# Gated DeltaNet mixer: triangular inverse without interleaving, convolutions in half-k passes, one 512-wide z weight, later correction chains; sliding-window mixer: v and the first q as one weight

## The chip, the cores and the metric

The kernel runs on one core of one Trainium2 chip. The metric is device time of one execution in microseconds (us). Engines are called as in the profile: PE multiplies matrices, DVE is the vector engine, ACT the scalar engine, POOL the GpSimd engine, SP issues the weight transfers. Each runs its instructions strictly in its own order, and semaphores tie the engines together.

## The reference

A trunk of two layers on 256 tokens of width 1024, each layer a half-weighted SwiGLU, a mixer, and another half-weighted SwiGLU. The mixer of layer 0 is a gated DeltaNet, that of layer 1 is sliding-window attention.

```python
def mixer_gated_deltanet(h, ...):
    proj = h @ w_in                       # q, k, v, z of 1024 columns each, b and a of 8
    qkv = silu(causal_depthwise_conv(qkv, w_conv))     # 4 taps along the tokens
    q = l2norm(q) * 128 ** -0.5 ; k = l2norm(k)        # 8 heads of 128
    beta = sigmoid(b) ; g = -exp(A_log) * softplus(a + dt_bias)
    o = gated_delta_rule_chunked(q, k, v, g, beta)
    return (rmsnorm(o, out_norm) * silu(z)) @ w_out

def gated_delta_rule_chunked(...):        # per chunk: decay = exp(g_i - g_j), i >= j
    L = where(strict, (kb @ k.T) * decay, 0)            # kb = k * beta
    u, w = solve_unit_lower(L, [v * beta, kb * exp(g)]) # the kernel builds the inverse
    v_new = u - w @ S ; o = q_dec @ S + ((q @ k.T) * decay) @ v_new
    S = S * g_last + k_dec.T @ v_new

def mixer_sliding_window_sinks(h, ...):   # 16 query heads of 64, 4 key/value heads
    proj = h @ w_in + b_in                # q 1024, k 256, v 256 columns
```

The kernel works with chunks of 128 tokens, so there are two (`t` is 0 or 1).

## The kernel before

**Weights.** Every weight is used in near fp32: SP loads a piece of 512 KB into `raw` (4 buffers), ACT casts it to `whi` (L310), and DVE subtracts, `wlo = raw - whi` (L312). For a few pieces POOL does that in four slices of 256 elements (L317); the argument `npool` says for how many of the two pieces of a 256-column weight. `whi` and `wlo` have 5 buffers each. A projection of 256 columns is two pieces: k (the contraction, in 8 blocks of 128) 0 to 3, and 4 to 7. Each block takes three matmuls: high by high, high by low, low by high (lines 363 to 365).

**PSUM.** `psA` has four banks and holds what is being accumulated by projections (`pcv` in the convolutions, `pz`, `acc`), `psB` four banks for the small products.

**Gated DeltaNet (`gdn`).** The order of the source is: z columns in chunks of 256 (`zproj`), the gates, then `conv` for k chunks 0 to 3, v chunks 0 to 3 and q chunks 0 to 3, where a chunk is 256 columns, two heads. A `conv` projects its two halves of 128 columns one after the other, each through all 8 blocks into a `pcv` bank. ACT copies the bank, scaled by the last tap, to `cv`; three *taps* on DVE (L928, on 255, 254 and 253 elements) read the bank and add to `cv`; ACT applies Silu. The bank is free after the third tap. Side work is written as generators and handed to a `Ticker`, which runs one step of it after each half of a `conv`.

The k chunks feed the *inverse*. `kpost` transposes k (`pkn`), sums its squares with four accumulating activations (`sumsq`, L721) and multiplies k by k (`pkk`) into `nf`. `blocks` cuts out the 32x32 diagonal blocks (`d`; ACT copies, POOL multiplications L768 and L770). `inverse` inverts 16x16 blocks on DVE, lines 780 to 818, all heads at once, and ends in `yx`. Two chains (`chain(0)` and `chain(1)`, four heads each) then go to 32, 64 and 128 rows by small matmuls (`pt`, `py`, `px`), each followed by a copy on ACT or DVE. The chains feed `u_of` and `state`. The tail takes four outputs `po` (chunk t, head group g) through `post` (square on ACT L1051, sum on DVE L1052, power on POOL L1055, scaling by four DVE instructions L1057 to `on`), `turn` (transpose `poT`, cast `oT`), and the output projection `acc`.

**Order.** A scheduler puts the written instructions of all engines in an order by its own estimates; `issue_after` and `keep_in_program_order` pin some of them.

**Sliding-window (`swa`).** v (`pv`) and q's first 256 columns (`pq`) are two weights of 256.

Of the kernel before, what the change touches and what calls it, by code (L numbers as in the profile page):

```python
# [15 lines left out]
P = 128  # L16
# [197 lines left out]
class Kern:  # L214
    def __init__(self, ctx, tc):
        self.tc = tc
        self.nc = tc.nc
        self.cp = ctx.enter_context(tc.tile_pool(name="const", bufs=1))
        self.wp = ctx.enter_context(tc.tile_pool(name="wts", bufs=5))
        self.bp = ctx.enter_context(tc.tile_pool(name="big", bufs=11))  # L220
        self.sp = ctx.enter_context(tc.tile_pool(name="small", bufs=2))
        self.pp = ctx.enter_context(
            tc.tile_pool(name="ps", bufs=4, space=bass.MemoryType.PSUM)
        )
        self.consts()
        self.hold = None
        self.early = None

# [59 lines left out]
    def split(self, src, hi, lo, shape, eng=None, cuts=1):  # L288
        nc = self.nc
        raw = self.wp.tile(shape, F32, tag="raw", name="raw", bufs=4)  # L290
        n = shape[1] // cuts
        parts = [slice(i * n, (i + 1) * n) for i in range(cuts)]
        if len(src.shape) == 4:
            for k in range(shape[1]):
                nc.sync.dma_start(out=raw[:, k].rearrange("p (g f) -> p g f", g=2), in_=src[:, k])
        else:
            nc.sync.dma_start(out=raw, in_=src)
        with ExitStack() as behind:
            if self.hold is not None:
                self.hold[0] -= 1  # L300
                if self.hold[0] < 0:
                    for ins in self.hold[2:]:
                        behind.enter_context(self.tc.issue_after(ins.ins))
                elif self.early is not None:
                    behind.enter_context(self.tc.issue_after(self.early.ins))
                self.hold[1] -= 1
                if not self.hold[1]:
                    self.hold = self.early = None
            for c in parts:
                nc.scalar.copy(hi[:, c], raw[:, c])  # L310
                if eng is None:
                    nc.vector.tensor_tensor(out=lo[:, c], in0=raw[:, c], in1=hi[:, c].bitcast(F32), op=ALU.subtract)  # L312
            if eng is not None:

                r, h, l = (a.rearrange("p a b -> p (a b)").rearrange("p (n f) -> p n f", f=256) for a in (raw, hi, lo))
                for i in range(4):
                    eng.tensor_tensor(out=l[:, i], in0=r[:, i], in1=h[:, i].bitcast(F32), op=ALU.subtract)  # L317
# [10 lines left out]
    def wcols(self, w, c0, npool=0):  # L328
        src = w[:, c0:c0 + 256].rearrange("(k p) f -> p k f", p=P)
        pieces = [self.wpiece(src[:, 4 * i:4 * i + 4, :], 4, 256,  # L330
                              eng=self.nc.gpsimd if i >= 2 - npool else None) for i in range(2)]
        return lambda k, cs: tuple(a[:, k % 4, cs] for a in pieces[k // 4])

    def wpairs(self, w, c0, between=None):
# [3 lines left out]
        for i in range(4):  # L338
# [4 lines left out]
            if between is not None and i == 1:  # L343
                between()
        return lambda k, cs: tuple(a[:, k % 2, cs] for a in pieces[k // 2])
# [34 lines left out]
    def proj_T(self, out, w, f, nrm):  # L380
        fs = slice(f * P, (f + 1) * P)
        for k in range(KT):
            wh, wl = w(k, fs)
            self.mm3(out, wh, wl, nrm.h.hi(k), nrm.h.lo(k), k == 0, k == KT - 1)
# [296 lines left out]
    def gdn(self, nrm, prep, w_in, w_out, after):  # L681
# [9 lines left out]
        tk = Ticker()  # L691
        Dt = self.big([P, NT, H, P], "Dt")
# [32 lines left out]
        def kpost(c):  # L725
# [3 lines left out]
            nc.scalar.copy(kd[:, hs, :], pv[:, 0])  # L729
            nc.scalar.copy(keg[:, hs, :], pv[:, 1])  # L730
            sumsq(pv, ssk, 2 * c)
            yield
            beta, eG, eS = res["beta"], res["eG"], res["eS"]
# [7 lines left out]
            a = ssk[:, :, hs]  # L741
            nc.vector.tensor_scalar_add(a, a, EPS)
            nc.vector.reciprocal(br[:, :, hs], a)
            nc.vector.tensor_mul(br[:, :, hs], br[:, :, hs], beta[:, :, hs])
            nc.vector.tensor_scalar_mul(nbr[:, :, hs], br[:, :, hs], -1.0)
            yield
            nc.gpsimd.tensor_tensor(out=kd[:, hs, :], in0=kd[:, hs, :], in1=bc(eS, 0, hs), op=ALU.mult)
            nc.gpsimd.tensor_tensor(out=keg[:, hs, :], in0=keg[:, hs, :], in1=bc(eG, 1, hs), op=ALU.mult)
# [7 lines left out]
        def blocks(g):  # L756
# [4 lines left out]
            us = slice(8 * g, 8 * g + 8)  # L761
            raw = self.y1([P, 8, 32], "d32")
# [6 lines left out]
            for j, m in enumerate(("tri16", "off16")):  # L769
                nc.gpsimd.tensor_tensor(out=d2[:, j, us, :], in0=raw,  # L770
                                        in1=M[m].unsqueeze(1).to_broadcast([P, 8, 32]), op=ALU.mult)
            nc.gpsimd.tensor_tensor(out=sv[:, :, gs], in0=ssk[:, :, gs],
                                    in1=self.phalf.rearrange("p (t h) -> p t h", t=NT), op=ALU.pow)

        def inverse():
# [21 lines left out]
            yield  # L797
# [13 lines left out]
            yield  # L811
# [6 lines left out]
            nc.vector.transpose(yx[:, 1].rearrange("p u c -> p (u c)"), yx[:, 0].rearrange("p u c -> p (u c)"))  # L818
            late["yx"] = yx
            tk.add(chain(0), chain(1))  # L820

        def chain(g):
# [6 lines left out]
            def blockwise(ps, lhsT, rhs):  # L829
                for i in range(8):  # L830
                    for b in range(4):
                        bs = slice(32 * b, 32 * b + 32)
                        nc.tensor.matmul(ps[bs, i * 32:i * 32 + 32], lhsT=lhsT[bs, i, :], rhs=rhs[bs, i, :],
                                         start=True, stop=True)
# [15 lines left out]
            for i in range(8):  # L850
                for b in (0, 2):
                    e, o = slice(32 * b, 32 * b + 32), slice(32 * b + 32, 32 * b + 64)
                    nc.tensor.matmul(pt[o, i * 32:i * 32 + 32], lhsT=nf[e, i, o], rhs=X[e, i, :], start=True, stop=True)
# [8 lines left out]
            for i in range(8):  # L862
                for b in (0, 2):
                    e, o = slice(32 * b, 32 * b + 32), slice(32 * b + 32, 32 * b + 64)
                    nc.tensor.matmul(py[e, i * 32:i * 32 + 32], lhsT=t32[o, i, :], rhs=Y[o, i, :], start=True, stop=True)
# [52 lines left out]
        def conv(col0, dst, npool, start):  # L918
            w = self.wcols(w_in, col0, npool)
            for f in range(2):  # L920
                ct = col0 // P + f
                ps = self.psA("pcv")
                self.proj_T(ps[:, :T], w, f, nrm)
                c = self.c1([P, T], "cv")
                nc.scalar.activation(c, ps[:, :T], AF.Copy, scale=wc[:, 3, ct:ct + 1])
# [5 lines left out]
                with self.tc.issue_after(res["exp"].ins):  # L931
                    nc.scalar.activation(dst(f), c, AF.Silu)
                tk.tick()
            tk.add(*start, first=True)

        def zproj(c, t, w):
            pz = self.psA("pz")
            self.proj_N(pz[:, :T], w, t, nrm)
            hs = slice(2 * c, 2 * c + 2)
            nc.scalar.copy(zs[:, t, hs, :], pz[:, :T].rearrange("p (h c) -> p h c", h=2))  # L940

        def zgate(t, hs, keep=lambda ins: ins):
            z = zs[:, t, hs]
            keep(nc.scalar.activation(z, z, AF.Silu))
            keep(nc.gpsimd.tensor_tensor(
                out=z, in0=z, in1=onb.unsqueeze(1).to_broadcast([P, hs.stop - hs.start, P]), op=ALU.mult))
# [7 lines left out]
        def then(*steps):  # L954
            for st in steps:
                r = st()
                if r is not None:
                    yield from r
                    yield

        w = [self.wcols(w_in, 3 * D + c * 256) for c in range(2)]
        zproj(0, 0, w[0])
        zproj(1, 0, w[1])
        tk.add(self.gdn_gates(nrm, wabh, wabl, expA, dtb, Dt, wq, res))
        tk.tick()
        for c in range(2):
            zproj(c, 1, w[c])
            tk.tick()
        zc = [2]

        def zmore(n):
            for c in range(zc[0], zc[0] + n):
                w = self.wcols(w_in, 3 * D + c * 256)
                for t in range(NT):
                    zproj(c, t, w)
                    tk.tick()
# [3 lines left out]
        for c in range(4):  # L980
# [5 lines left out]
            conv(D + c * 256, lambda f: kT[:, 2 * c + f, :], c // 2, [then(*steps)])  # L986
# [94 lines left out]
        for c in range(4):  # L1081
# [5 lines left out]
            if c == 2:  # L1087
                n = 2 * zc[0]
                w = self.wcols(w_in, 3 * D + 3 * 256)
                for t in range(NT):  # L1090
                    zproj(3, t, w)
                    zgate(t, slice(n, H))
                    tk.tick()
        tk.drain()
# [53 lines left out]
    def swa(self, nrm, prep, w_in, w_out, after):  # L1148
# [9 lines left out]
        wv = self.wcols(w_in, D + 256)  # L1158
        w0 = self.wcols(w_in, 0)
        for t in range(NT):  # L1160
            ts = slice(t * P, (t + 1) * P)
            ps = self.psA("pv")
            self.proj_N(ps[:, :T], wv, t, nrm)
            nc.vector.tensor_add(v[:, t, :], ps[:, :T], bv)
            ps = self.psA("pq")
            self.proj_N(ps[:, :T], w0, t, nrm)
            qn = self.c1([P, T], "qn")
            nc.scalar.copy(qn, ps[:, :T])
            pt = self.psB("pqt")
# [205 lines left out]
```

## Time and profile before

| | |
|---|---|
| three runs, us | 1018.77, 1019.48 (median), 1020.96 |
| the profiled execution's own time, us | 1017.73 |
| its span, first to last instruction, us | 1016.0 |
| mean granted TensorE clock | 0.996 |
| busy: PE, DVE, ACT, POOL | 98%, 63%, 54%, 24% |
| gated DeltaNet, first `pz` matmul to the first matmul of the next SwiGLU, us | 195.39 to 368.90 |

All times on the trace's clock are us from the span's start. In a timeline row the first number is the start, the second how long it took; matmuls overlap, so the distance between starts says how long PE was held. The square bracket tells how long the engine stood idle before and for whom. PEclk is the clock granted to PE as a share of full speed.

### The profile page before, as it was taken

The page shows a single profiled execution, that of the slowest core. Times are in us where ns is not written, and L with a number is a line of the kernel's source. Part 1 is how long each engine was busy: PE and PEld are TensorE (multiplying, and loading weights), DVE is VectorE, ACT ScalarE, POOL GpSimd, SP SyncE. Part 2 cuts the span into 40 slices and gives each one's busy share as a digit, 9 for nine tenths or more (in the row PEclk, how much of TensorE's full clock was granted, in tenths as well). Part 3 has the DMA queues.
Part 4 walks back from the last instruction along what each step waited for, and adds up shares of the span by engine and source line. Part 5 has one row for each costly group of instructions (what it writes and reads, how often), then busy time and mean ns, then how long its engine had stood idle before and what let it go on. Part 6 is the DMA issues. An engine that isn't in the chain of part 4 may idle for free.

```text
span 1016.0 us, 16483 instructions
## 1 busy us (share of the span) xinstructions
PE 998.0 (98%) x6195; PEld 870.7 (86%) x6195; DVE 643.7 (63%) x975; ACT 547.8 (54%) x979; POOL 242.1 (24%) x311
## 2 busy tenths in 40 slices
PE   8999999999989999999999999999999999999997
PEld 7888888899979888888888888888898678888886
DVE  5866654666895766666546666664578756666544
ACT  5756544457856445555434655553467545555442
POOL 0125510017952301323100123320021402222100
PEclk9999999999999999999999999999999999999999
DMA  7766666644452337666666666665563426666661
GB/s 246 235 188 191 200 197 182 205 129 148 133 175 65 105 104 208 195 188 197 191 199 190 186 187 186 192 207 189 185 209 104 152 91 212 190 189 187 203 188 43
DMA packets 135316, 177.05 MB, mean 174 GB/s; under 512 B 7250, under 2 KB 120260, under 8 KB 135236
## 3 DMA queue, kind: packets, MB, share of 16 engines
q1 hardware_dynamic: 132032, 171.46, 55.3%
q10 hardware_dynamic: 3204, 4.53, 1.4%
q8 instruction: 49, 0.80, 0.3%
q14 instruction: 31, 0.25, 0.1%
HBM read 174.92 MB, written 1.05 MB: 173 GB/s over the span
## 4 chain that ended last, share of the span: by engine, by line
PE 89%; DVE 4%; ACT 3%; issue 1%; DMA 1%; POOL 1%; SPq 1%; POOLq 0%; ACTq 0%
PE pg L370 14%; PE pu L370 14%; PE acc L365 9%; PE acc L363 9%; PE acc L364 9%; PE pu L371 7%; PE pg L371 7%; PE pgu L365 2%; PE pgu L364 2%; PE pgu L363 2%; DVE wlo L312 1%; DMA raw<-in_ffn_w_gu_dram 1%; PE pcv L363 1%; PE pcv L364 1%; PE pcv L365 1%
## 5 line engine op out<-in xcount | busy, mean ns | idle before, releaser
L312 DVE TENSOR_TENSOR wlo<-raw,whi 128x1024 fp32r<-128x1024 f32 (+1 forms) x304 | 374.9, 1236 | 198.0 <-ACT whi L310 196.8
L310 ACT CAST whi<-raw 128x1024 fp32r<-128x1024 f32 (+1 forms) x318 | 330.3, 1046 | 179.5 <-PE acc L365 83.2
L370 PE MATMUL pg<-hs,whi 128*128 128x512 f32 x624 | 218.7, 392 | 0.0
L370 PE MATMUL pu<-hs,whi 128*128 128x512 f32 x624 | 218.4, 392 | 0.0
L371 PE MATMUL pu<-hs,wlo 128*128 128x256 f32 x624 | 175.4, 281 | 0.0
L371 PE MATMUL pg<-hs,wlo 128*128 128x256 f32 x624 | 174.6, 281 | 0.0
L478 POOL TENSOR_TENSOR act<-act,gate 128x256 f32<-128x256 f32 x78 | 58.6, 751 | 352.0 <-DVE act L477 337.4
L370 PEld LDWEIGHTS pg<-hs,whi 128*128 128x128 f32 x624 | 116.9, 187 | 25.3
L370 PEld LDWEIGHTS pu<-hs,whi 128*128 128x128 f32 x624 | 116.9, 187 | 25.2
L364 PE MATMUL acc<-wlo,ah 128*128 128x512 f32 (+1 forms) x340 | 128.6, 378 | 0.0
L365 PE MATMUL acc<-whi,al 128*128 128x512 f32 (+1 forms) x340 | 128.5, 378 | 0.0
L363 PE MATMUL acc<-whi,ah 128*128 128x512 f32 (+1 forms) x340 | 128.0, 378 | 0.0
L371 PEld LDWEIGHTS pg<-hs,wlo 128*128 128x128 f32 x624 | 118.2, 189 | 0.4
L371 PEld LDWEIGHTS pu<-hs,wlo 128*128 128x128 f32 x624 | 118.2, 189 | 0.0
L363 PEld LDWEIGHTS acc<-whi,ah 128*128 128x128 f32 x340 | 64.0, 188 | 12.0
L364 PEld LDWEIGHTS acc<-wlo,ah 128*128 128x128 f32 x340 | 64.0, 188 | 11.8
L365 PEld LDWEIGHTS acc<-whi,al 128*128 128x128 f32 x340 | 64.0, 188 | 11.9
L481 POOL TENSOR_SCALAR ah<-act 128x256 fp32r<-128x256 f32 x78 | 66.4, 852 | 6.7
L467 ACT COPY gate<-pg 128x256 f32<-128x256 f32 x78 | 28.7, 368 | 55.6 <-PE pg L371 55.6
L476 ACT COPY act<-pu 128x256 f32<-128x256 f32 x78 | 28.7, 368 | 54.1 <-PE pu L371 54.1
L363 PE MATMUL pcv<-hs,whi 128*128 128x256 f32 x192 | 55.1, 287 | 2.2 <-DVE cv L928 2.2
L99 POOL TENSOR_TENSOR rst<-var,mhalf 128x1 f32<-128x1 f32 x10 | 5.6, 557 | 215.6 <-DVE var L97 215.6
(340 smaller groups left out, 1576.6 us busy)
## 6 DMA issues: line engine op xcount, KB each, us to landing
raw<-in_ffn_w_gu_dram SPq DMA_DIRECT2D x156, 512.0 KB, 4.4
raw<-in_ffn_w_down_dram SPq DMA_DIRECT2D x88, 512.0 KB, 4.2
raw<-in_a_w_in_dram SPq DMA_DIRECT2D x32, 512.0 KB, 4.2
raw<-in_ffn_w_gu_dram SPq DMA_DIRECT2D x40, 256.0 KB, 4.7
raw<-in_b_w_in_dram SPq DMA_DIRECT2D x12, 512.0 KB, 4.8
raw<-in_a_w_out_dram SPq DMA_DIRECT2D x8, 512.0 KB, 3.7
raw<-in_b_w_out_dram SPq DMA_DIRECT2D x8, 512.0 KB, 3.7
nw<-in_ffn_norm_dram ACTq DMA_DIRECT2D x3, 512.0 KB, 4.0
```

Of the source, the lines that this page charges most:

```text
L99: nc.gpsimd.tensor_tensor(out=r, in0=v, in1=k.mhalf[:, 0:1], op=ALU.pow)
L310: nc.scalar.copy(hi[:, c], raw[:, c])
L312: nc.vector.tensor_tensor(out=lo[:, c], in0=raw[:, c], in1=hi[:, c].bitcast(F32), op=ALU.subtract)
L363: nc.tensor.matmul(out, lhsT=lh, rhs=rh, start=start, stop=False)
L364: nc.tensor.matmul(out, lhsT=lh, rhs=rl, start=False, stop=False)
L365: return nc.tensor.matmul(out, lhsT=ll, rhs=rh, start=False, stop=stop)
L370: nc.tensor.matmul(out, lhsT=lh, rhs=r2, start=start, stop=False)
L371: return nc.tensor.matmul(out[:, :T], lhsT=ll, rhs=rh, start=False, stop=stop)
L467: nc.scalar.copy(g, pg[:, T:])
L476: nc.scalar.copy(a, pu[:, T:])
L478: nc.gpsimd.tensor_tensor(out=a, in0=a, in1=gates[f], op=ALU.mult)
L481: ahead[2] = nc.gpsimd.tensor_scalar(oh, a, 1.0, None, op0=ALU.mult)
```

## The change

1. z chunks 0 and 1 become one weight of 512 columns (`wide`): four pieces of two k blocks, and 48 matmuls of 512 columns in place of 96 of 256. In the other mixer v and q's first 256 columns become one weight in the same manner (its pieces come as two transfers each), one bank `pqv`.
2. `conv` takes both halves' banks at once and goes through k in two passes: half 0 blocks 0 to 3, half 1 blocks 0 to 3, half 0 blocks 4 to 7, half 1 blocks 4 to 7. The taps follow the second pass. z chunks 2 and 3 do the same.
3. `sumsq` is one ACT square of 128x512 and one DVE reduction. The two copies of k become one. The small arithmetic for `knbr` moves from each chunk to each pair of chunks (`blocks`), the scaling of k by gates (`kscale`, 8 POOL instructions) moves behind the POOL subtractions of v chunk 2.
4. `inverse` has no yields. The taps of v chunk 1 are pinned behind its last transpose (`late["inv"]`).
5. The chains get tickers of their own (`tkc`), start with v chunk 2, and their matmuls are pinned behind the latest convolution matmul (`late["mm"]`).
6. z chunk 3 moves from behind q chunk 2 to behind v chunk 0. The z gate's POOL multiplications are cut into pieces of 256.
7. POOL's subtractions: k chunks 1 and 2 one piece each, z chunk 3 one, v chunk 0 none, v chunk 1 both (pinned behind the second `blocks`' masks), v chunks 2 and 3 and the q chunks one each. The second power `ks` is pinned behind v chunk 1's subtractions.

```diff
+    def wide(self, w, *c0):
+        n = 512 // len(c0)
+        src = [w[:, c:c + n].rearrange("(k p) f -> p k f", p=P) for c in c0]
...
+        for i in range(4):
...
+            self.split(parts if len(parts) > 1 else parts[0], hi, lo, [P, 2, 512])
...
         def sumsq(pv, ss, h0):
-            for i in range(2):
-                for t in range(NT):
-                    j = self.small([P, P], "junk", 1)
-                    nc.scalar.activation(j, pv[:, t, i, :], AF.Square, accum_out=ss[:, t, h0 + i:h0 + i + 1])
+            nc.scalar.activation(pv, pv, AF.Square)
+            nc.vector.tensor_reduce(out=ss[:, :, h0:h0 + 2], in_=pv, axis=AX.X, op=ALU.add)
...
-            nc.vector.transpose(yx[:, 1].rearrange("p u c -> p (u c)"), yx[:, 0].rearrange("p u c -> p (u c)"))
+            late["inv"] = nc.vector.transpose(yx[:, 1].rearrange("p u c -> p (u c)"),
+                                              yx[:, 0].rearrange("p u c -> p (u c)"))
             late["yx"] = yx
-            tk.add(chain(0), chain(1))
...
-        def conv(col0, dst, npool, start):
+        def conv(col0, dst, npool, start, behind=None):
             w = self.wcols(w_in, col0, npool)
-            for f in range(2):
-                ct = col0 // P + f
-                ps = self.psA("pcv")
-                self.proj_T(ps[:, :T], w, f, nrm)
...
+            acc = [self.psA("pcv") for f in range(2)]
+            for half in range(2):
+                for f in range(2):
+                    late["mm"] = self.proj_T(acc[f][:, :T], w, f, nrm, range(4 * half, 4 * half + 4))
+                    tkc[f].tick()
+                    if half:
+                        taps(col0 // P + f, acc[f], dst(f), behind)
+                        tk.tick()
...
-            conv(D + c * 256, lambda f: kT[:, 2 * c + f, :], c // 2, [then(*steps)])
+            conv(D + c * 256, lambda f: kT[:, 2 * c + f, :], int(c in (1, 2)), [then(*steps)])
...
-            conv(2 * D + c * 256, lambda f: vT[:, f, :], 1, [vpost(c, vT)])
+            self.masks = late["d"] if c == 1 else None
+            conv(2 * D + c * 256, lambda f: vT[:, f, :], ((), (0, 1), (1,), (1,))[c], [vpost(c, vT)],
+                 late["inv"] if c == 1 else None)
+            if c == 0:
+                zmore(1)
+            if c == 1:
+                roots(1, self.short)
+            if c == 2:
+                late["short"] = self.short
+                for g in range(2):
+                    tkc[g].add(chain(g))
+                tk.add(kscale())
...
-        wv = self.wcols(w_in, D + 256)
-        w0 = self.wcols(w_in, 0)
+        w0 = self.wide(w_in, 0, D + 256)
```

On DVE, the first third of the inverse before: taps and a weight's subtraction stand between its instructions.

```order
L780 STREAM_TRANSPOSE tw<-d_2607 128x512
L783 TENSOR_TENSOR inv<-tw 128x256
L312 TENSOR_TENSOR wlo<-raw,whi 128x1024
L784 COPY inv<-inv 128x256
L928 SCALAR_TENSOR_TENSOR cv<-pcv,wc,cv 128x255
L785 MEMSET inv 128x16
L793 TENSOR_TENSOR itmp<-inv 128x8
L928 SCALAR_TENSOR_TENSOR cv<-pcv,wc,cv 128x254
L796 TENSOR_TENSOR inv<-inv,itmp 128x4x2
L928 SCALAR_TENSOR_TENSOR cv<-pcv,wc,cv 128x253
```

On DVE, the end of the inverse and what follows it in the changed kernel; L850 is the inverse's last transpose, L975 are the taps (of v chunks 1 and 2), L318 a weight's subtraction.

```order
L843 TENSOR_REDUCE inv<-tw 128x8x8
L844 COPY tw<-inv 128x512
L847 STREAM_TRANSPOSE tw<-tw 128x16x32
L848 TENSOR_TENSOR yx<-tw,blk_953 128x512
L318 TENSOR_TENSOR wlo<-raw,whi 128x1024
L850 STREAM_TRANSPOSE yx<-yx 128x512
L975 SCALAR_TENSOR_TENSOR cv<-pcv,wc,cv 128x255 x4
L975 SCALAR_TENSOR_TENSOR cv<-pcv,wc,cv 128x254 x4
L318 TENSOR_TENSOR wlo<-raw,whi 128x1024
L975 SCALAR_TENSOR_TENSOR cv<-pcv,wc,cv 128x253 x4
```

The inverse, over which five subtractions and twenty taps were spread, holds two subtractions and no tap now; the third taps of v chunk 1, which free its two banks, stand behind eight other taps and a subtraction.

On DVE, the tail before: the sums (`so`), factors (`fo`) and scalings (`on`) of the last three outputs `po`; `on_3948` and `on_3968` belong to the first two, `so_4013` to the third, and the transposes on PE wait for `on`.

```order
L1052 TENSOR_REDUCE so_3947<-on_3948 128x4
L1052 TENSOR_REDUCE so_3967<-on_3968 128x4
L1054 TENSOR_TENSOR fo_3951<-ssq_1913,so_3947 128x4
L1054 TENSOR_TENSOR fo_3971<-ssq_1913,so_3967 128x4
L1057 SCALAR_TENSOR_TENSOR on_3948<-po_3942,fo_3951,zs_1905 128x128 x4
L1057 SCALAR_TENSOR_TENSOR on_3968<-po_3958,fo_3971,zs_1905 128x128 x4
L1052 TENSOR_REDUCE so_4013<-on_4014 128x4
```

The same place now; `on_3841` and `on_3861` belong to the first two outputs, `so_3906` to the third.

```order
L1114 TENSOR_REDUCE so_3840<-on_3841 128x4
L1114 TENSOR_REDUCE so_3860<-on_3861 128x4
L1116 TENSOR_TENSOR fo_3844<-ssq_1913,so_3840 128x4
L1116 TENSOR_TENSOR fo_3864<-ssq_1913,so_3860 128x4
L1114 TENSOR_REDUCE so_3906<-on_3907 128x4
L1119 SCALAR_TENSOR_TENSOR on_3841<-po_3835,fo_3844,zs_1905 128x128 x4
L1116 TENSOR_TENSOR fo_3910<-ssq_1913,so_3906 128x4
L318 TENSOR_TENSOR wlo_4075<-raw_4076,whi_4074 128x1024
L1119 SCALAR_TENSOR_TENSOR on_3861<-po_3851,fo_3864,zs_1905 128x128 x4
```

The third output's sum has moved ahead of the first output's scaling, and a weight's subtraction ahead of the second's.

On PE, the same stretch before, from the last matmuls of a run of eight `acc` on; the third output is `po_4004`, and `poT` transposes the first two.

```order
L363 MATMUL acc_3979<-whi_3910,oT_3228 128x512
L364 MATMUL acc_3979<-wlo_3911,oT_3228 128x512
L365 MATMUL acc_3979<-whi_3910,oT_3228 128x512
L1004 MATMUL po_4004<-S_3227,wq_1907 128x128
L1004 MATMUL po_4004<-u_2634,Dt_1904 128x128
...
L1065 MATMUL poT_4024<-ident_70,on_3948 128x128 x4
L1065 MATMUL poT_4031<-ident_70,on_3968 128x128 x4
L363 MATMUL acc_3978<-whi2_3919,oT_3228 128x512
```

Now, from the last matmuls of the second output on; the third is `po_3897`.

```order
L1066 MATMUL po_3851<-u_2540,Dt_1904 128x128
L1066 MATMUL po_3835<-u_2540,Dt_1904 128x128 x2
L1066 MATMUL po_3897<-S_3150,wq_1907 128x128
L1066 MATMUL po_3897<-u_2540,Dt_1904 128x128
...
L1127 MATMUL poT_3917<-ident_70,on_3841 128x128 x4
L386 MATMUL acc_3871<-whi2_3812,oT_3151 128x512
```

The eight `acc` have moved ahead of the outputs: between the second output and the first `poT` stand only the eight matmuls of the third.

More of the change, by code (lines that the diff above doesn't have):

```diff
@@ L691, in gdn @@
         tk = Ticker()
+        tkc = [Ticker() for g in range(2)]
         Dt = self.big([P, NT, H, P], "Dt")
@@ L1086, in gdn @@
                 tk.add(then(first))
[L1087 to L1094, printed above, removed]
+        for ticker in (*tkc, tk):
+            ticker.drain()
         ws = self.out_weights(w_out, (3, 4))
```

151 lines of the change are left out of this document (93 added, 58 removed).

## The prediction

> **What bounds the kernel now.** I read the engines' shares first, then the mixer by windows, then the waits of PE. Two lines of the page, the second the weight transfers of this mixer (KB each, us from issue to landing):
>
> ```profile
> PE 998.0 (98%) x6195; PEld 870.7 (86%) x6195; DVE 643.7 (63%) x975; ACT 547.8 (54%) x979; POOL 242.1 (24%) x311
> ...
> raw<-in_a_w_in_dram SPq DMA_DIRECT2D x32, 512.0 KB, 4.2
> ```
>
> PE is the bound, so a change pays if it shortens PE's own work or PE's waits. The windows of PE over the gated DeltaNet mixer (us, busy, clock) show where it waits; busy time counts work at a lower clock in full.
>
> ```profile
> 195.39:270.98 75.59, 75.21 (x606) 1.00 0.45 139
> 270.98:306.66 35.68, 31.01 (x476) 0.95 0.54 173
> 306.66:348.79 42.13, 41.66 (x475) 1.00 0.27 78
> 348.79:368.90 20.11, 19.45 (x95) 1.00 0.32 103
> ```
>
> Only 270.98 to 306.66 is loose, and only there is the clock below 1. PE's timeline shows the waits, the two windows under it the clock:
>
> ```profile
> 194.69 0.39 PE L363 MATMUL acc<-xhi,ah 128*128 128x512 f32 x1
> 194.92 0.40 PE L364 MATMUL acc<-xlo,ah 128*128 128x512 f32 x1
> ...
> 283.05 0.28 PE L364 MATMUL pcv<-hs,whi 128*128 128x256 f32 x1
> 283.17 0.28 PE L365 MATMUL pcv<-hs,wlo 128*128 128x256 f32 x1
> 284.95 0.36 PE L363 MATMUL pcv<-hs,whi 128*128 128x256 f32 x1 [1.50 <-DVE cv L928]
> ...
> 291.64 0.36 PE L363 MATMUL pcv<-hs,whi 128*128 128x256 f32 x1 [0.70 <-DVE cv L928]
> ...
> 297.63 1.31 PE L833 MATMUL pt<-yx,d 32*32 32x32 f32 x128 [0.49 <-DVE yx L818]
> ...
> 301.51 1.83 PE L833 MATMUL py<-yx,t 32*32 32x32 f32 x128 [1.98 <-ACT t L837]
> ...
> 303.87 0.41 PE L364 MATMUL pz<-wlo,hs 128*128 128x256 f32 x1
> 304.08 0.41 PE L365 MATMUL pz<-whi,hs 128*128 128x256 f32 x1
> ...
> 307.82 0.25 PE L853 MATMUL pt<-X,nf 32*32 32x32 f32 x5 [0.47 <-DVE X L844]
> ...
> 302.00:303.00 1.00, 1.00 (x87) 0.50 0.86 307
> 305.00:306.00 1.00, 1.00 (x9) 0.81 0.00 0
> ```
>
> A matmul of 256 columns holds PE .12 us, one of 512 .23. Twice a `conv` waits for its bank, whose taps lag on DVE; then the chain waits for `yx` and `t`, and after the wait of 1.98 the granted clock is half for about 3.4 us (matmuls every .21).
>
> Why the taps and `yx` are late, DVE, POOL and ACT show:
>
> ```profile
> 271.47 1.11 DVE L780 STREAM_TRANSPOSE tw<-d 128x512 f32<-128x512 f32 x1 [0.35 <-POOL d L770]
> 271.47:297.57 26.10, 26.06 (x49) 1.00 0.54 169
> 271.47:297.57 26.10, 8.54 (x20) 1.00 0.54 169
> 271.47:297.57 26.10, 8.26 (x5) 1.00 0.54 169
> 273.04 1.75 DVE L312 TENSOR_TENSOR wlo<-raw,whi 128x1024 fp32r<-128x1024 f32 x1
> 282.00 1.05 DVE L805 TENSOR_TENSOR tw<-inv 128x512 f32<-128x512 f32 x1
> 291.41 1.21 DVE L312 TENSOR_TENSOR wlo<-raw,whi 128x1024 fp32r<-128x1024 f32 x1
> 293.69 2.87 DVE L312 TENSOR_TENSOR wlo<-raw,whi 128x1024 fp32r<-128x1024 f32 x1
> 261.88 0.16 DVE L743 RECIPROCAL kbr<-ssk 128x4 f32<-128x4 f32 x1
> 256.11 1.65 POOL L772 TENSOR_TENSOR ks<-ssk,phalf 128x8 f32<-128x8 f32 x1 [1.40 <-DVE ssk L742]
> 267.40 2.64 POOL L772 TENSOR_TENSOR ks<-ssk,phalf 128x8 f32<-128x8 f32 x1
> 270.70 0.73 POOL L770 TENSOR_TENSOR d<-d,tri 128x256 f32<-128x256 f32 x1
> 272.09 6.84 POOL L317 TENSOR_TENSOR wlo<-raw,whi 128x256 fp32r<-128x256 f32 x8
> 293.18 2.30 POOL L945 TENSOR_TENSOR zs<-zs,onb 128x768 f32<-128x768 f32 x1
> 259.87 1.64 ACT L765 COPY d<-nf 32x256 f32<-32x256 f32 x4
> 277.73 1.05 ACT L310 CAST whi<-raw 128x1024 fp32r<-128x1024 f32 x1
> 330.39 0.60 ACT L1051 ACTIVATE on<-po 128x512 f32<-128x512 f32 x1 [0.29 <-PE po L1004]
> ```
>
> The second to fourth rows are DVE in the inverse's stretch: in all, its taps (L928), its subtractions (L312). DVE is full for 26.1 us, and 26.06 − 8.54 − 8.26 = 9.3 us of that are the inverse itself.
>
> **The change part by part.**
>
> Two passes per `conv`, merged copies, the z gate in pieces and the chains' pins add no work to PE: a weight's second piece is needed 1.4 us later (12 matmuls), and both banks come free later. 0, except where they make the waits below. The squares go from eight short ACT instructions to one of .6 (the last row above) and a sum on DVE of .7, counted below.
>
> Wide weights: 48 pairs of .12 become 48 of .23: 48 × .01 = .5 us saved, and as much in the second mixer: −1.0 (0 to −1.2). The four more transfers there, of half the size, stand in SP's queue ahead of its next weights; the transfer of such a piece takes 4.2 us while PE works on earlier ones, and I cost them at 0; if that cover were short, PE would wait once at the mixer's start.
>
> Before the inverse: the cumulated waits of PE were 1.2 us by 270.98 (its 606 matmuls at their spacings against 75.59); fewer squares on ACT, and banks taken in pairs, leave about half: −.6 (0 to −1).
>
> The inverse starts earlier. In PE's new order the last k transposes and products stand so that, adding up matmuls at their spacings from 195.39 and .6 of wait, they end at 256.2. Behind them on DVE: the product with the mask and the new reduction (.7 each, like the sum over 512 elements quoted for the tail), two taps (.43 each, 8.54 / 20), four small steps (.16 each); ACT's copies of blocks, 1.64, run beside these; then two steps of POOL (.73 each). That is 260.5, instead of 271.47.
>
> What stands behind it. DVE now does 9.3 us (rows above, where taps filled the gaps between dependent steps) to 12.8 (the same rows end to end); I take 12, since every step needs the one before. With two subtractions (1.21 and 1.4) it ends at 275.1 instead of 297.6. Eight taps follow (3.4), to 278.5, then a subtraction (1.21), then v chunk 1's first third tap (.43): 280.1.
>
> The new wait. v chunk 3's first matmul needs that bank, and the subtraction ahead of the third tap is for a weight piece whose `raw` buffer POOL frees with v chunk 2's last slice. POOL: masks to 261.2, eight slices 6.84, the power 2.1 (1.65 and 2.64 in the rows), four slices 3.4: 273.5. Then landing 4.2, cast 1.05, subtraction 1.21, tap .43: 280.4, and DVE's own path gives 280.1: both agree. PE's matmuls up to v chunk 3 end at 273.0, and its last low-part matmul needs POOL's last slice as well: 273.7. So PE stands still 6.7 us. Bounds: 5.2 (POOL's work .85 as long, 278.2 against 273.0) and 8.1 (the inverse at 12.8 and its subtractions at 1.75 each). z chunk 3's 96 matmuls, moved ahead, are what covers the inverse; without them the wait would be 11.5 longer. Its SP loads, casts and subtractions move with it ahead of v chunk 1's, whose last POOL slice, at 268.0, comes 2 us before PE's matmul that needs it: 0. So do the eight scalings of k behind v chunk 2's slices: `state` needs them some 20 us later.
>
> After the wait the clock halves, as after 1.98 us before: 3.4 us at half, 1.6 lost (bounds 1.5 and 1.8). [...]
>
> What goes: by starts less spacings the waits at 284.95, 291.64, 297.63 and 301.51 cost 1.7, .9, .6 and 2.2, the halved clock 1.7, the step at 307.82 .6: −7.7. From there to 348.79 the sum of spacings leaves another 1.0, which falls to about .3, since eleven or more matmuls (1.3 us) now stand between the chain's steps: −.7. What covers the steps now are v chunk 3 and q chunks 0 and 1; where a step comes late, PE waits for it again.
>
> The tail. Rows of it:
>
> ```profile
> 345.32 1.36 DVE L1052 TENSOR_REDUCE so<-on 128x4 f32<-128x512 f32 x2 [1.67 <-ACT on L1051]
> 347.86 2.16 DVE L1057 SCALAR_TENSOR_TENSOR on<-po,fo,zs 128x128 f32<-128x128 f32 x8 [0.99 <-POOL fo L1055]
> 348.79 1.62 PE L1065 MATMUL poT<-ident,on 128*128 128x128 f32 x8
> 351.06 0.50 PE L363 MATMUL acc<-whi,oT 128*128 128x512 f32 x1 [0.65 <-ACT oT L1068]
> ```
>
> Before, `poT` lost 1.62 − .9 = .7 and `acc` .65: 1.4. Now eight `acc` (1.8 us of cover) have gone from in front of the third output, and its sum stands ahead of the first output's scaling on DVE: from the second output's end the third output 1.8, square .6, sum .68, four scalings 1.08, signals .3: 4.5 against PE's 1.8, a wait of 2.7; then .65 for `oT` as before and .5 for the second output behind a subtraction (1.21) and four scalings: 3.9, so +2.5 (bounds +.5, where the scheduler's neighbours run early, and +3.3 with the clock halved there too).
>
> Sum: −1.0 − .6 − 7.7 − .7 + 6.7 + 1.6 + 2.5 = +.8. The profiled execution took 1017.73, 1.75 under the median; so 1018.5 on its own clock, and 1020.3 against the median of 1019.48. A measurement tells .2% (2.0 us) from no change, so this is no change: one large wait for several.
>
> **The rivals.**
>
> Faster. The bank is free at 278.2 (POOL's path at its shortest, DVE at 9.3 to 11 for the inverse), and the tail loses .5 more than before instead of 2.5. That is −1.5 and −2.0: 1016.8. For it speaks the power's row of 1.65; against it the eight slices at 6.84, and the order in the tail, in which the waits follow on each other.
>
> Slower, on the other side: POOL holds up the inverse. While DVE runs the inverse in one go, POOL runs twelve slices, each with two inputs from SBUF. The subtraction at 293.69 took 2.87 beside a POOL multiplication of 2.30 that had begun .51 earlier, and 1.21 at 291.41: 1.66 more, nearly to POOL's end. The one at 273.04 beside slices took 1.75, .54 more. [...] Against it: the product at 282.00, of 512 elements and beside slices, took 1.05. Some eight of the inverse's instructions have two such inputs; at .35 (between 0 and .54) that is 2.8 us, the bank comes free at 282.9, the wait is 9.2: 1022.8. At a whole slice each (6.84 / 8 = .86) it would be 6.9, and 1026.9. It decides once it adds over 1.5 us, where the sum leaves the .2%.
>
> That the wait is short enough for the clock to stay up (under 1.5, as at 284.95): −6.8, 1013.5, for which both paths above would have to be 5 us too long.
>
> **How the numbers follow.** No change by the sum: .42. Shorter waits: .33, of which .05 is the far end. Held-up inverse: .25. The likeliest alone spans 1017.5 to 1021.5. The range takes both rivals in: 1014.5 to 1023.5, which leaves out about .15, the 1013.5 and the 1026.9 among it.
>
> **What would show it.** Right: DVE begins the inverse near 260 and ends near 275; PE waits some 6 to 7 us near 273 for a tap; the clock is .5 behind that; the first `poT` of the last group waits over 2 us. Wrong: no wait above 4 us near 273, or products of the inverse longer than their rows here (1.05 and 1.12 for 512 elements).

## The result, and the profile after

The changed kernel is slower: 1027.49 us median of four runs (1026.91 to 1029.16) against 1019.97 (1018.77 to 1020.96); the ratio is 1.0079, with a 95% interval of 1.0063 to 1.0095. The profiled execution of the changed kernel took 1027.27, that of the kernel before 1017.73, so the two traces differ by 9.5 us, 2 more than the medians: the trace of before is a quick one. All of it lies in the gated DeltaNet mixer, 183.97 us long instead of 173.51; the second mixer is .75 shorter (85.75 to 85.00), and the rest agrees within .1.

The windows of PE over the mixer in the changed kernel (us, busy, clock), cut at the one long wait, at the end of the half clock behind it, and at the tail:

```profile
195.20:265.00 69.80, 69.51 (x519) 1.00 0.43 133
265.00:284.30 19.30, 8.76 (x67) 0.86 0.44 136
284.30:289.20 4.90, 4.90 (x24) 0.52 0.69 217
289.20:354.20 65.00, 65.00 (x897) 1.00 0.37 115
354.20:379.17 24.97, 22.45 (x96) 0.86 0.22 70
```

The second row is the damage: PE works 8.76 us of 19.30. PE's timeline names what ended the wait, and the two waits of the tail; the last two rows are windows of the clock:

```profile
284.12 0.55 PE L386 MATMUL pcv<-hs,whi 128*128 128x256 f32 x1 [9.40 <-DVE cv L975]
284.48 0.41 PE L387 MATMUL pcv<-hs,whi 128*128 128x256 f32 x1
...
356.36 1.01 PE L1127 MATMUL poT<-ident,on 128*128 128x128 f32 x4 [1.84 <-DVE on L1119]
358.05 0.79 PE L386 MATMUL acc<-whi,oT 128*128 128x512 f32 x1 [0.68 <-ACT oT L1130]
...
358.00:359.00 1.00, 0.95 (x2) 0.50 0.00 0
363.00:364.00 1.00, 1.00 (x4) 0.50 0.00 0
```

It is the wait that was forecast, on the tap that was forecast, at the place forecast (273.7; here 274.4), only longer: 9.6 us by starts, not 6.7. The clock falls to half inside it, at 278.8, and stays there until 289.0; in the tail it is half from 357.3 to 364.1. The inverse on DVE, with POOL beside it:

```profile
261.42 1.09 DVE L814 STREAM_TRANSPOSE tw<-d 128x512 f32<-128x512 f32 x1 [1.33 <-POOL d L798]
264.47 0.67 DVE L830 TENSOR_TENSOR inv<-inv,itmp 128x8 f32<-128x8 f32 x1
265.17 0.66 DVE L827 TENSOR_TENSOR itmp<-inv 128x8 f32<-128x8 f32 x1
266.55 1.42 DVE L838 TENSOR_TENSOR tw<-inv 128x64 f32<-128x64 f32 x2
268.15 0.42 DVE L841 TENSOR_TENSOR tw<-iw,inv 128x64 f32<-128x64 f32 x2
272.06 1.57 DVE L841 TENSOR_TENSOR tw<-iw,inv 128x512 f32<-128x512 f32 x1
278.66 0.70 DVE L850 STREAM_TRANSPOSE yx<-yx 128x512 f32<-128x512 f32 x1
282.38 1.21 DVE L318 TENSOR_TENSOR wlo<-raw,whi 128x1024 fp32r<-128x1024 f32 x1
283.51 1.64 DVE L975 SCALAR_TENSOR_TENSOR cv<-pcv,wc,cv 128x253 f32<-128x253 f32 x4
262.04 5.84 POOL L326 TENSOR_TENSOR wlo<-raw,whi 128x256 fp32r<-128x256 f32 x8
269.47 4.70 POOL L326 TENSOR_TENSOR wlo<-raw,whi 128x256 fp32r<-128x256 f32 x4
```

The inverse runs from 261.42 to 279.36, 17.9 us, where 14.6 were forecast. While POOL's eight slices run (one in .73), each product of DVE, of 8 or of 64 elements, takes about as long as one slice: .57 for the first, .66 to .71 (half of 1.42) for the five behind it. Each ends .02 to .08 us after a slice does. When the slices end, at 267.88, two products of 64 elements take .42 together; the two before took 1.42.

### The profile page after: what moved, and what is told of

Same layout as the page of the kernel before. It is cut to its first block, busy times and chain, and to the rows that moved or that the text cites. A ratio compares the mean times of both kernels' runs of the same rounds, so it can differ in the third digit from the quotient of the medians.

```text
span 1025.6 us, 16237 instructions
## 1 busy us (share of the span) xinstructions
PE 1000.8 (98%) x6099; PEld 868.1 (85%) x6099; DVE 650.8 (63%) x974; ACT 543.8 (53%) x915; POOL 248.7 (24%) x319
## 3 DMA queue, kind: packets, MB, share of 16 engines
HBM read 174.92 MB, written 1.05 MB: 172 GB/s over the span
## 4 chain that ended last, share of the span: by engine, by line
PE 93%; DVE 3%; DMA 1%; issue 1%; ACT 1%; POOL 0%; SPq 0%; POOLq 0%; ACTq 0%; DVEq 0%
PE pg L393 14%; PE pu L393 14%; PE acc L386 9%; PE acc L388 9%; PE acc L387 9%; PE pu L394 7%; PE pg L394 7%; PE pcv L386 2%; PE pcv L387 2%; PE pcv L388 2%; PE pgu L388 2%; PE pgu L387 2%; PE pgu L386 2%; DVE wlo L318 1%; PE psc L1252 1%
## 5 line engine op out<-in xcount | busy, mean ns | idle before, releaser
L318 DVE TENSOR_TENSOR wlo<-raw,whi 128x1024 fp32r<-128x1024 f32 (+1 forms) x303 | 373.4, 1236 | 193.3 <-ACT whi L316 191.8
L326 POOL TENSOR_TENSOR wlo<-raw,whi 128x256 fp32r<-128x256 f32 x60 | 49.4, 854 | 40.8 <-ACT whi L316 40.8
```

Of the source, the lines that this page charges most:

```text
L326: self.short = eng.tensor_tensor(out=l[:, i], in0=r[:, i], in1=h[:, i].bitcast(F32), op=ALU.subtract)
```

## The experiments

The question was which part makes the wait long: POOL beside the inverse (theory A), the inverse's own dependent steps (theory B), the pin on the taps, the tail's order, or the clock. Ratios are to the kernel before on the same chip. The changed kernel was not run again beside the experiments, so two versions are compared by their ratios; the changed kernel's is 1.0079.

**1. POOL writes and does not read beside the inverse.** v chunk 1's POOL subtractions become memsets, three for each:

```diff
-    self.short = eng.tensor_tensor(out=l[:, i], in0=r[:, i], in1=h[:, i].bitcast(F32), op=ALU.subtract)
+    for _ in range(3):
+        self.short = eng.memset(l[:, i].bitcast(F32), 0.0)
```

> The changed kernel with POOL's eight subtractions for v chunk 1, which run beside the inverse, replaced by three times as many memsets of the same tile (POOL stays busy and writes, but reads nothing; the low part of that weight is left out). Theory A, POOL's reads of SBUF hold up DVE's instructions with two SBUF inputs: the inverse's first third, from its first transpose to the first 512-element product, falls from 7.3 us to about 5, the inverse in all from 17.9 to 15 to 16 us (four more POOL subtractions stay beside its end), PE's wait at the bank from 9.4 to 6 to 7, and the time to 1022 to 1024.5. Theory B, DVE's small dependent instructions take as long as they took whatever POOL does: 17.5 to 18 us for the inverse, 9 to 9.5 for the wait, 1027.

1028.64 us, ratio 1.0101 (1.0086 to 1.0116): slower still by the median, though the intervals overlap, and neither theory's number: the inverse takes 20.6 us, and PE waits 11.4 for the bank. The first two rows are DVE's, then POOL's memsets and power, then DVE behind them:

```profile
262.38 0.42 DVE L822 TENSOR_TENSOR inv<-tw 128x256 f32<-128x256 f32 x1
262.84 5.30 DVE L823 COPY inv<-inv 128x256 f32<-128x256 f32 x1
261.83 6.16 POOL L329 MEMSET wlo<- 128x256 f32 x24
267.93 1.71 POOL L811 TENSOR_TENSOR ks<-ssk,phalf 128x8 f32<-128x8 f32 x1
268.38 0.17 DVE L835 TENSOR_TENSOR inv<-inv,itmp 128x8 f32<-128x8 f32 x1
268.59 0.17 DVE L832 TENSOR_TENSOR itmp<-inv 128x8 f32<-128x8 f32 x1
```

Beside memsets the product of 256 elements took .42, but the copy behind it stood still until the last of them had ended: 5.30 us. Then products of 8 elements took .17 beside a POOL power. So B falls (steps of .17 by themselves), and A has to be widened: POOL's slices held up DVE's products (.66 for .17), POOL's memsets held up a DVE copy (5.30), and a power over 8 elements held up no product (.17).

**2. POOL idle beside the inverse.** The low parts of v chunks 1 to 3 that POOL computed are left out; a tile of zeros stands in the same matmuls.

```diff
+        if self.zero and eng is not None:
+            lo = self.zlo
         self.split(src, hi, lo, [P, a, b], eng)
...
+            self.zero = c > 0
```

> The changed kernel in which POOL does nothing beside the inverse but one power: the low parts of v chunks 1 to 3 that it would compute are left out, and a tile of zeros takes their place in the same matmuls. [...] Theory B (dependent small instructions in a run take that long by themselves): .5 to .7 for 8 elements, over 16.5 us for the inverse.

1022.57, ratio 1.0043 (1.0028 to 1.0058). DVE:

```profile
263.55 1.12 DVE L819 STREAM_TRANSPOSE tw<-d 128x512 f32<-128x512 f32 x1 [1.62 <-POOL d L803]
265.05 1.22 DVE L321 TENSOR_TENSOR wlo<-raw,whi 128x1024 fp32r<-128x1024 f32 x1
266.71 0.17 DVE L835 TENSOR_TENSOR inv<-inv,itmp 128x8 f32<-128x8 f32 x1
267.32 0.45 DVE L843 TENSOR_TENSOR tw<-inv 128x64 f32<-128x64 f32 x2
271.44 1.12 DVE L846 TENSOR_TENSOR tw<-iw,inv 128x512 f32<-128x512 f32 x1
277.08 0.69 DVE L855 STREAM_TRANSPOSE yx<-yx 128x512 f32<-128x512 f32 x1
```

The inverse takes 14.2 us, two taps included, close to the forecast's 14.6; products of 8 elements take .15 to .17, the first two of 512 take 1.05 and 1.12, and a third of 512 took 1.22 at 275.54, beside POOL's slices for q chunk 0 (273.23 to 276.2). POOL's work beside the inverse is therefore worth at least 3.7 us of its length, and some .8 more for the two taps. It begins 2.1 us later here (POOL's order ahead of it differs), and PE's wait is 5.7 by starts, 3.9 less. Not all of that is the inverse: it ends 1.6 earlier (277.78 against 279.36), and the tap that frees the bank stands behind three taps and a subtraction instead of eight and one, 2.0 us less, and PE came to it .3 later.

**3. No pin on v chunk 1's taps.**

```diff
-                 late["inv"] if c == 1 else None)
+                 None)
```

> The changed kernel without the pin that holds v chunk 1's taps behind the inverse's last transpose. If the order of DVE (eight taps and a subtraction ahead of the third tap) is what makes the wait long: the bank is free some 5 us earlier, PE's wait is 4 to 5 us instead of 9.4, and the time 1021 to 1023.5. If the inverse itself holds DVE until the end whatever the pin: a wait of 8 to 9 us and 1026 to 1027.

1021.85, ratio 1.0044 (1.0026 to 1.0061). PE's waits, the largest (total, times, longest):

```profile
PE pcv L386 <- DVE cv L975: 5.5, 1, 5.5
PE poT L1127 <- DVE on L1119: 1.8, 1, 1.8
```

The taps go between the last steps of the inverse, and the wait falls by 3.9. The mixer's length falls by 6.6 in this trace (177.39); some 3 of these are the tail's half clock, which did not come in this execution. By the ratios, .0035 of the .0079 that was lost comes back, from one line.

**4. The tail's order of before.** This version was to hold eight `acc` between the second and third output; the third output's sum is pinned behind the first two's scalings.

```diff
+        with self.tc.issue_after(last.ins):
+            held = self.out_part(acc[1], ob[0], ws, 1, range(1, 4))
+        with self.tc.issue_after(held.ins):
+            o_of(1, 1)
...
+        self.early = post(1, 1, res["on"])
```

> The changed kernel with the tail's order of before: eight output-projection matmuls held between the second and third output, and the third output's sum on DVE pinned behind the first two's scalings. If the tail's order costs what the trace shows there (a wait of 2.0 and .9, and 6.7 us at half clock behind it, some 3.3): the clock stays up in the tail and the time falls by 4 to 5.5, to 1022 to 1023.5. If the wait in the tail only moves (the outputs being late for another reason): 1026 to 1027.5.

1025.78, ratio 1.0077 (1.0062 to 1.0092), which is the changed kernel's. PE's waits in the tail, and under them its order there:

```profile
PE poT L1132 <- DVE on L1124: 1.4, 1, 1.4
...
PE acc L388 <- DVE oT L1136: 0.7, 1, 0.7
...
351.75 0.39 PE L1066 MATMUL po<-u,Dt 128*128 128x128 f32 x2
351.90 0.48 PE L386 MATMUL acc<-whi,oT 128*128 128x512 f32 x1
...
353.60 0.60 PE L1066 MATMUL po<-u,Dt 128*128 128x128 f32 x4
353.96 0.48 PE L387 MATMUL acc<-wlo,oT 128*128 128x512 f32 x1
354.27 0.40 PE L388 MATMUL acc<-whi,oT 128*128 128x512 f32 x1
354.51 0.38 PE L1066 MATMUL po<-S,wq 128*128 128x128 f32 x2
...
357.84 1.01 PE L1132 MATMUL poT<-ident,on 128*128 128x128 f32 x4 [1.38 <-DVE on L1124]
```

The waits stay: the first `poT` waits 1.4 instead of 1.8, a later `acc` .7 more, and the sum by starts is 3.3 against 2.9. But the order of before did not come back on PE. Seven of the nine `acc` stand ahead of the last matmuls of the first two outputs (353.60), where they cover nothing, and only two behind. The time from the last start of these outputs to the first `poT` is 3.9 us in both (353.93 to 357.84; in the changed kernel 352.45 to 356.36). Before, eight `acc` and the third output filled that time; in the changed kernel the third output alone does, 1.9 us, and the wait is 2.0; here they are 2.3 and 1.6. So the missing cover, which the forecast blamed, does account for the first wait. The third output's sum does not: with it behind the scalings (run 4) the 3.9 stays 3.9. No version here brought all eight `acc` back.

**5. Both, 3 and 4.**

> The changed kernel without the pin of v chunk 1's taps and with the tail's order of before. If both losses are separate and add: the run without the pin was 1021.9, the one with the tail's order 1.7 under the changed kernel, so 1020 to 1021. If the tail's gain was only the clock not falling there (which the run without the pin has already): 1021.5 to 1022.5.

1022.30, ratio 1.0040 (1.0026 to 1.0054), no better than 3 alone: the second alternative's number. Its reason is not shown: the mean granted clock of the profiled execution was .993 here and in run 4, and .996 in run 3.

**6. The half clock.** 36 multiplications of the identity in front of v chunk 3, first behind the transposes of v on PE, then directly behind v chunk 2's last matmul:

```diff
+    with self.tc.issue_after(late["mm"].ins):
+        for _ in range(36):
+            fill = nc.tensor.matmul(ps[:, 0:P], lhsT=self.ident, rhs=self.ident, start=True, stop=True)
```

> The changed kernel with 36 idle matmuls of the identity (7.9 us by their spacing of .22) placed on PE in front of v chunk 3's first matmul, inside the wait; their result is not used. If the half clock behind the wait is a cost of its own: the wait at the bank ends when it ended, the clock is full behind it, and the time falls by 2 to 2.6 us (5 us at half clock in the changed kernel), to 1025. If the clock falls anyway, or the time at half clock was hidden by other waits: 1027 to 1028.

1035.29, ratio 1.0165 (1.0149 to 1.0180): a transpose that waits 9.8 us for v chunk 1's Silu stood ahead of them, so they ran behind the wait and cost the 7.9 us that they take (1027.5 + 7.9 = 1035.4). It tells nothing of the clock, but that PE has no slack there.

> The changed kernel with the 36 idle matmuls of the identity (7.9 us) directly behind v chunk 2's last matmul on PE, ahead of the transposes and of v chunk 3, so that they fall into the wait (in the run before, they stood behind a transpose that waits for the same taps, and cost their whole 7.9 us). If the half clock behind the wait is a cost of its own: the bank comes free when it did, the clock is full behind it, and the time is 2 to 2.6 us under the changed kernel, 1025. If it is not: 1027 to 1028.

1025.20, ratio 1.0065 (1.0048 to 1.0082), by the ratios some 1.4 us under the changed kernel, though the intervals overlap. The trace is clearer: the mixer takes 181.76 us instead of 183.97, the bank comes free as before (284.48 against 284.12), matmuls follow every .12 where they followed every .21, and the window behind is at full clock.

```profile
284.48 0.36 PE L386 MATMUL pcv<-hs,whi 128*128 128x256 f32 x1 [1.36 <-DVE cv L989]
284.67 0.28 PE L387 MATMUL pcv<-hs,whi 128*128 128x256 f32 x1
284.79 0.28 PE L388 MATMUL pcv<-hs,wlo 128*128 128x256 f32 x1
287.00:288.00 1.00, 1.00 (x36) 1.00 1.09 384
```

**7. v chunk 1's subtractions moved.** Both on DVE, then one on each engine without the pin:

```diff
-            conv(..., ((), (0, 1), (1,), (1,))[c], [vpost(c, vT)],
+            conv(..., ((), (), (1,), (1,))[c], [vpost(c, vT)],       # first
+            conv(..., ((), (1,), (1,), (1,))[c], [vpost(c, vT)],     # second, and masks for c in (1, 2), no pin
```

> The changed kernel with both subtractions for v chunk 1 on DVE instead of POOL. Theory A: products of the inverse take their undisturbed lengths (about .4 for 8 elements, 1.1 for 512), but DVE has two more subtractions of 1.2 us and the scheduler puts taps between the inverse's instructions again, so the inverse's stretch is 18 to 20 us and PE's wait at the bank 4 to 8 us; 1020 to 1026. Theory B: as long per instruction as with POOL, a stretch of over 22 us, 1027 to 1030.

1037.08, ratio 1.0186 (1.0171 to 1.0201), slower than either expectation. The first `masks` pin had gone with the POOL slices: four slices of v chunk 2 (2.8 us), the eight scalings of k that follow them (5.6) and four slices of v chunk 3 (3.8) came ahead of the masks on POOL, and the inverse began at 273.23, 12 us later. A product of 512 elements that began while POOL stood idle took 1.05; beside slices the first three of 8 elements took .67, .37 and .38. The second product of 512 took 1.14 beside slices, and there POOL's work was the longer: four slices took 4.76 beside it and a subtraction (1.71), where four took 2.84 at 259.76. PE waited three times for banks, 10.2 us in all.

> The changed kernel with one of v chunk 1's two subtractions on DVE and one on POOL, v chunk 2's POOL subtraction kept behind the masks, and no pin on v chunk 1's taps. If the wait at the bank was made of POOL's locks and of the taps' place behind the inverse: less of both, a wait of 2 to 4.5 us (5.7 in the run without the pin), and the time 1018.5 to 1021. If DVE's one more subtraction takes back what the four slices less give: 1021 to 1023.

1024.38, ratio 1.0067 (1.0049 to 1.0085), above both expectations. The wait at the bank is 3.0, less than the 5.5 of run 3, and yet the median is longer: PE then waits 1.7 in a chain step, and the clock falls behind the wait and in the tail again (half for 5 and for nearly 7 us). The chain's wait and the tail's half clock, which run 3 did not have, take more than the bank's wait gives.

**8. The last quarter of the inverse behind the taps**, the chains a convolution later:

```diff
+                while h == 8 and "tap" not in late:
+                    yield
...
+                            later.enter_context(self.tc.issue_after(late["tap"].ins))
```

> The changed kernel with the last quarter of the inverse (from the sum of the first 512-element product on) pinned behind v chunk 1's taps, in place of the taps behind the inverse, and the chains started one convolution later. If the bank is what PE waits for near 273: the wait there falls from 9.4 to under 2.5 us, the clock stays at full, and the time falls by 8 to 11 to 1016.5 to 1019.5. If PE then waits as long for the inverse's result: the wait moves to the chain's first product (3 to 6 us) and the time is 1021 to 1025.

1022.99, ratio 1.0052 (1.0036 to 1.0069). The later chains put the first output's product (320.05) ahead of the update of `u` that it should read (334.70), so its time is only a hint. PE's wait for the bank is 1.0, and three others take its place:

```profile
PE pcv L388 <- POOL wlo L326: 3.1, 2, 2.4
PE pvn L739 <- issue: 2.6, 1, 2.6
...
PE pws L1075 <- DVE S L1097: 1.2, 1, 1.2
```

**9. The wide weights on the kernel before**, both, and then the second mixer's alone:

```diff
-        wv = self.wcols(w_in, D + 256)
-        w0 = self.wcols(w_in, 0)
+        w0 = self.wide(w_in, 0, D + 256)
```

> The kernel before with only the two wide weights (z chunks 0 and 1 as one of 512 columns, v and q's first as one). If 48 matmuls of 512 columns in place of 96 of 256 are worth their spacings: .5 us in each mixer, 1.0 in all, so 1017.0 against a median of 1018.0 in this job's earlier runs, unless the scheduler moves other waits. If the wider pieces come late (each needs all 512 columns of two blocks before the first matmul): no change or up to 1 us slower.

1020.40, ratio 1.0022 (1.0011 to 1.0032): slower. The scheduler puts the transposes of k differently, and PE waits for ACT's copies and squares, where it waited for nothing:

```profile
251.09 0.41 PE L732 MATMUL pkn<-ident,kT 128*128 128x128 f32 x2 [1.29 <-ACT kk L748]
252.95 0.80 PE L757 MATMUL pkk<-kT 128*128 128x128 f32 x2 [1.45 <-ACT junk L739]
```

The changed kernel, where the squares are one instruction, does not have these waits.

> The kernel before with only the second mixer's wide weight (v and q's first 256 columns as one of 512), where nothing else changes its place on any engine. The term of the prediction by itself: 48 matmuls of 512 columns for 96 of 256 are worth .5 us by their spacings, and .75 by the stage's length in the changed kernel's trace (85.00 us against 85.75). So a stage of 85.0 to 85.3 us and a median .5 to .8 us under the kernel before. If the wider pieces, two transfers each, come late for the first matmul: a stage of 85.75 or longer.

1017.05, ratio .9990 (.9972 to 1.0008). The stage takes 85.00 us, as in the changed kernel, against 85.75; the ratio agrees but can't be told from 1. It is the only version here whose median lies under both kernels'.

## Why the prediction was wrong, point by point

It forecast no change, about .8 us more, and gave the slower case .25; the time lies above its range. The place and the side of each term were right, and so was the trade of several waits for one. The inverse's length was wrong by a mechanism that it had set aside as a rival, and the sizes of five terms err the same way. By the traces:

| term | forecast, us | measured, us | from |
|---|---|---|---|
| wide weights | −1.0 | −.75 and about −.6 | stage 85.75 to 85.00; spacings |
| waits before the inverse | −.6 | −.7 | starts over the usual spacings, to 283.1 before and to 270 now |
| waits and half clock that go | −8.4 | −6.6 | the same: 11.6 from 283.1 to 348.8 before, 5.0 from 289.0 to 354.2 now |
| wait at the bank | +6.7 | +9.6 | by starts |
| waits for POOL's slices ahead of it | 0 | +1.5 | .85 and .61 by starts |
| half clock behind it | +1.6 | +2.2 | 284.1 to 289.0; run 6 |
| tail | +2.5 | +4.7 | waits of 2.9 for 1.5; half clock some 3 |

The sum is about 9.3, against 9.5 between the traces. The usual spacing is the median distance between starts of one kind of matmul.

- **The inverse's length** is the step that failed, and the largest single miss: "I take 12, since every step needs the one before". With POOL idle beside nearly all of it, that was right (run 2: 14.2 with subtractions and taps against 14.6). The rows that I took came from an inverse that taps stood between, and a tap met no delay (.39 from start to start beside slices); a run of products beside a run of POOL slices did. The held-up inverse was my rival, and its first size was nearly right: eight instructions at .35, 2.8 us, a wait of 9.2, 1022.8. In the trace six products lost .42 to .50 each (.57 to .71 against .15 to .22), 2.9 us, and a copy between them .4 (.71 against .28). That the far end of this rival, 1026.9, is close to the measured time is luck: it reckoned with 6.9 us more inverse and a wait of 13. The longer wait alone (+2.9) would have left the time at 1023.2, inside the range; the tail, the waits for slices and the waits that stayed took it out. I let one row decide: the product at 282.00, beside slices and undisturbed. The collision was there too, and POOL paid for it; the slice that started with this product took 1.60 instead of .73:

```profile
281.99 1.60 POOL L317 TENSOR_TENSOR wlo<-raw,whi 128x256 fp32r<-128x256 f32 x1
```

- **POOL's path and DVE's agreed** in the forecast at 280.1 to 280.4. They parted: v chunk 2's slices ended at 274.2 (forecast 273.5), the third tap on DVE was 3.9 late (283.98), and only the later one counts. The inverse ended 4.2 late, 3.3 by its length and .9 by its start (261.42 for 260.5; the POOL multiplication ahead of it took 1.46 beside a subtraction on DVE, .62 in run 2), and the taps behind it made up .3. The wait of .7 for POOL's last slice stood in the forecast's place (273.7 for 273.0) and not in its sum.
- **The clock.** I took 3.4 us at half for any wait. Behind the 9.6 it was 4.9 us, and in the tail 6.8, where I allowed for it in the bound alone. The last section has the lengths that were measured; what sets them is not shown.
- **The tail's waits** were forecast at 3.9 and came to 2.9. The missing cover was right, the path behind it was too long: 3.9 us from the outputs to the first `poT` where I had 4.5, as the third output's sum is not on it (run 4).
- **The waits that go** saved 6.6 and not 8.4: 5.0 us over the usual spacings remain among the chain's steps. Which of them I had wrong stays open.
- **The pin** was counted in the path to the bank (eight taps and a subtraction), but not seen as what to change: without it alone 3.9 of the wait goes. No run has both the pin and POOL's slices away, so it is not shown how much of the wait would be left.

## What to carry to other kernels

Price a run of dependent short vector instructions by what runs beside it as well as by its rows: here products of 8 elements took .66 beside POOL slices of .73, and .17 without. When several small waits are traded for one, add the clock that falls behind a long one: here 4.9 us of work at half behind a wait of 9.6, 2.2 us lost. And ask of each pin what stands behind the pinned instruction: here four taps kept two banks from PE.

## What the runs showed of the hardware

- In the changed kernel products of 8 elements on DVE, with two inputs from SBUF, took .57 to .67 beside POOL's subtraction slices of .72 to .79, and each ended .02 to .03 after a slice; with POOL's slices away (run 2) they took .15 to .17. POOL's side grew too: in the kernel before, a product of 512 elements that started with a slice (282.00) took 1.05, and that slice 1.60 instead of .73. A POOL power over 8 elements, 1.7 us long, did not hold up products of .17 (run 1).
- A copy of 256 elements on DVE took .28 beside no slice (run 2), .71 beside slices (the changed kernel), and 5.30 beside 24 memsets in a row on POOL (run 1), where it ended .15 after the last of them. A product of 256 elements beside the same memsets took .42.
- In the changed kernel the clock changed at 278.77, 289.01, 357.28 and 364.10: 10.24, 68.27 and 6.83 us apart, which are 3, 20 and 2 times the 3.41 us for which it was half in the kernel before (301.97 to 305.38). Of the other stretches at half whose two ends were read, that in the tail of run 1 lasted 3.4 us, and those of run 2 at the bank, of the second version of 6 in the tail and of the second of 7 at the bank and in the tail 6.8 each.
- The tail of the changed kernel waited 2.0 and .9 us by starts. Six kernels whose clock was read there have these same two waits (1.8 and .7 in the profile's brackets), and the clock fell behind them in four (the changed kernel, run 1, the second version of 6 and the second of 7, for 3.4 or 6.8 us) and not in two (runs 2 and 3). So the wait's length alone did not settle it; what did is not shown. Each of these is one profiled execution, so how often the clock falls in one kernel stays open.
